# Modulation rows of a transformer layer in unsplit float32, on four 32-column tiles of the matmul array

## The chip, the cores and the metric

One core of one Trainium2 chip runs the whole kernel. A core has a matmul engine (TensorE, PE in the profile, with its weight loads as PEld), VectorE (DVE), ScalarE (ACT), GpSimd (POOL), and queues of transfers that move data between HBM and the on-chip memory SBUF; here SyncE (SP) issues nearly all transfers. Matmuls write to PSUM, which has eight banks. The metric is the time of one execution on the device in microseconds (us).

## The reference

One layer of a diffusion backbone over 256 latent tokens and 256 context tokens of width 2048, all in float32. Both token sets are normalised and modulated by scales and shifts that a large matrix makes from a conditioning vector, then projected, mixed and sent through an MLP. What concerns the change is the start:

```python
mod = (jax.nn.silu(c) @ w_mod[l] + b_mod[l])[:, None, :]
sa, ca, ga, sm, cm, gm = jnp.split(mod, 6, axis=-1)
mod_c = jax.nn.silu(c_ctx) @ w_mod[l] + b_mod[l]
sa_c, ca_c, ga_c, sm_c, cm_c, gm_c = jnp.split(mod_c, 6, axis=-1)
h_c = modulate(x_ctx, norm_attn_w[l], sa_c, ca_c)      # rmsnorm(x) * (1 + scale) + shift
h = modulate(x, norm_attn_w[l], sa, ca)
p = h @ w_in[l]                                        # Q, K, V, pooling input, gates
```

The scale and shift before attention (`ca`, `sa`) are needed for both conditioning vectors: 2048 x 4096 weights by two vectors. `ga`, `sm`, `cm`, `gm` are needed for the latent tokens alone and are made later on VectorE. After the projection come attention of 8 heads with two softmaxes each, a pooling branch, gates, an output projection with a residual, and an MLP of width 8192.

## The kernel before, in words

Float32 operands of most matmuls are split in two: ScalarE rounds a weight chunk to the reduced format float32r (`whi`, L213), VectorE subtracts (`wlo`, L214), and three matmuls at the speed of the reduced format (hi by hi, lo by hi, hi by lo) replace one in full float32 (`mm3`, L241 to L243; `xstat`, L410 to L413). A chunk is 128 x 1024 numbers, 512 KB. It lands in one of five `raw` buffers (`raw_chunk`, L113), and the next transfer into that buffer is issued when its last reader is through.

`plan` writes down one list of all chunks, the stream; `wchunk` takes the next and has `load_next` bring chunks from it `ahead` places early. Each engine runs its own instructions in order; a scheduler interleaves them at build time.

The front of the program goes as follows. The tokens `xT` land; sums of squares (L459 to L461: square on ScalarE, add, a float32 matmul with a constant) give the norms. Then come the modulation weights `w_m`, in feature groups `m` of 256 features (the first in two halves). `mod_chunk` (L347) takes a chunk: the stationary operand is `cv`, 128 columns wide, of which four are not zero (hi and lo of the two conditioning vectors), and the moving operand is 512 columns of `whi`, then of `wlo`. After all of K = 2048, `mod_rows` (L352) copies four rows out of PSUM, `mod_columns` turns them into columns by transposes (L359), copies those (L361), adds hi and lo (L365) and applies biases and the norm's weight (L367 to L369). `hidden` (L380 to L382) makes the modulated tokens of that group, `hL` for latent and `hC` for context tokens, as hi and lo.

While modulation chunks stream in, the first half of the K and Q projections runs beside them as side work: `first_steps` yields three matmuls at a time, and the table `carried` says at which chunk of which group the K chunk for latent tokens ("kx"), for context tokens ("kc") or the Q chunk ("q") is begun. When all 16 feature tiles are done, the rest of K and Q follows, and then V (`xstat`), with the evacuations `qk_evac` beside it. Behind that stand the second half of Q, K and V, pooling, gates, attention (its score matmuls at L646, its products with V at L674), the output projection and the MLP. None of these is touched.

Of the kernel before, what the change touches and what calls it, by code (L numbers as in the profile page):

```python
# [11 lines left out]
F32 = mybir.dt.float32  # L12
F32R = mybir.dt.float32r
# [35 lines left out]
def layer(ctx: ExitStack, tc, a, out):  # L49
# [74 lines left out]
    def plan(name, *idx, rate=0.0):  # L124
# [3 lines left out]
    carried = {1: ((1, "kx", 0), (4, "q", 0)), 2: ((2, "kx", 1), (4, "q", 1)),  # L128
               3: ((0, "kc", 0), (3, "kx", 2), (5, "q", 2), (6, "kc", 1))}
    for m in range(4, 8):  # L130
        carried[m] = ((0, "kc", m - 2), (2, "kx", m - 1), (4, "q", m - 1))
    carried[8] = ((0, "kc", 6), (0, "kx", 7), (0, "q", 7), (0, "kc", 7))
    for m in range(9):
        if m == 0:
            for half in range(2):
                for i in range(4):
                    plan("w_m0", half, i)
        for i in range(8 if m > 0 else 0):
            if m < 8:
                plan("w_m", m - 1, i)  # L140
            for at, n, j in carried[m]:
                if at == i and n != "kc":
                    plan("w_k" if n == "kx" else "w_q", 0, j)
            if m == 1 and i > 5 or m == 2 and i < 2:
                plan("cT", (8 * m + i - 14))
            if m == 3 and i == 4:
                plan("prq")
# [29 lines left out]
    AHEAD = 2  # L177
    x1s = []
# [10 lines left out]
    def load_next():  # L189
# [14 lines left out]
        raw = raw_chunk(src, n)  # L204
        if key[:2] == ("w_k", 0):
# [134 lines left out]
    def mod_chunk(key, i, ps, n):  # L340

        hi, lo = wchunk(*key, i)
        per = 1024 // n
        for part in (hi, lo):
            for kk in range(per):
                k = per * i + kk
                pe.matmul(ps[:, 0:n], cv[:, k, :], part[:, kk * n:kk * n + n], start=(k == 0 and part is hi),  # L347
                          stop=(k == 15 and part is lo))

    def mod_rows(ps, n=512):  # L350
        rows = work("rows", [4, n])
        act.copy(rows, ps[0:4, 0:n])  # L352
        return rows

    def mod_columns(k, rows, n=2):
# [10 lines left out]
        ks = slice(k, k + n)  # L366
# [97 lines left out]
    kept = {}  # L464
    fb = {}

    def first_steps(n, j):
# [4 lines left out]
        if n == "kc":  # L472
            hi, lo = kept.pop(j)
        else:
            hi, lo = wchunk(w, 0, j)
            if n == "kx":
                kept[j] = hi, lo
# [7 lines left out]
    def steps(g, n):  # L485
        for _ in range(n):
            next(g, None)
# [5 lines left out]
    cols = {}  # L493
    for half in range(2):
        ps = bank("mod")
        for i in range(4):
            mod_chunk(("w_m0", half), i, ps, 256)
            if half == 1 and i == 1:
                cols[0] = mod_columns(0, rows, 1)
                hidden(0, 0, cols[0], 1)  # L500
        rows = mod_rows(ps, 256)
# [590 lines left out]
```

## Time and profile before

| what | value |
|---|---|
| median of 3 runs | 1520.16 us (1519.46 to 1521.07) |
| the profiled execution's own time | 1519.78 us |
| its span, first to last instruction | 1517.7 us |
| granted TensorE clock, mean | 0.994 |
| moved between HBM and SBUF | 347.82 MB, mean 229 GB/s |

The profile is of one execution. "Busy" is the time in which an engine had at least one instruction under way; matmuls overlap one another, so PE's busy time is more than what it streams. A group's row names the line, the engine, the operation, output from inputs, shape and type, then the count, the busy time and the mean length of one in ns, then the engine's idle time before such instructions with what ended it. The line of a helper stands for all that call it. A row of a wait names the waiting engine and line, what it waited for, the total, the number of times and the longest.

### The profile page before, as it was taken

To read this page: it belongs to the slowest core of one execution; us is meant where nothing else is said; L and a number is where in the kernel's file an instruction comes from. 1 tells how busy PE (TensorE), PEld (TensorE's weight loads), DVE (VectorE), ACT (ScalarE), POOL (GpSimd) and SP (SyncE) were. 2 spreads that over 40 slices of the span, in tenths; PEclk is the share of its full clock that TensorE was granted. 3 is DMA by queue.
4 is the path that set the end of the run, shared out by engine and by line. 5 is a ranking of instruction groups with operands and counts; after the bars stand their busy time and mean duration, and the time that the engine had idled before them with its cause. 6 is when DMAs were issued, how large, how long until landed. Compare 5 with 4: busy or idle time off the path is not lost.

```text
span 1517.7 us, 19767 instructions
## 1 busy us (share of the span) xinstructions
PE 1480.7 (98%) x7336; PEld 1232.8 (81%) x7336; DVE 1063.2 (70%) x1280; ACT 755.7 (50%) x1007; POOL 129.3 (9%) x124
## 2 busy tenths in 40 slices
PE   7899999999989999999999999999999999999998
PEld 5677877768878888888879988888888888888887
DVE  7799878777887767666757665666666555555675
ACT  6677534556655444444444554544444454444432
POOL 0100111000140000000000100100000000000170
PEclk9899999999999999999999999999999999999999
DMA  8888668556568787788755677767777666666664
GB/s 314 310 283 308 214 215 285 177 167 193 167 216 300 254 275 272 242 295 296 235 181 168 220 251 245 232 217 244 231 241 240 202 188 193 193 187 193 184 200 142
DMA packets 97439, 347.82 MB, mean 229 GB/s; under 512 B 11072, under 2 KB 11712, under 8 KB 97344
## 3 DMA queue, kind: packets, MB, share of 16 engines
q1 hardware_dynamic: 96768, 345.49, 70.4%
q8 instruction: 57, 0.93, 0.3%
q0 software_dynamic: 576, 1.08, 0.2%
q14 instruction: 38, 0.31, 0.1%
HBM read 344.44 MB, written 2.10 MB: 228 GB/s over the span
## 4 chain that ended last, share of the span: by engine, by line
PE 88%; issue 3%; DVE 3%; DMA 3%; ACT 1%; POOL 1%; DVEq 0%; SPq 0%; ACTq 0%; POOLq 0%
PE f L939 14%; PE f L411 8%; PE f L410 8%; PE f L413 8%; PE f L942 7%; PE pg L413 4%; PE pg L410 4%; PE pg L411 4%; PE pyy L410 2%; PE wo L410 2%; PE wo L413 2%; PE wo L411 2%; PE pyy L413 2%; PE pyy L411 2%; PE v L411 2%
## 5 line engine op out<-in xcount | busy, mean ns | idle before, releaser
L214 DVE TENSOR_TENSOR wlo<-raw,whi 128x1024 fp32r<-128x1024 f32 x507 | 628.6, 1244 | 365.2 <-ACT whi L213 350.9
L213 ACT CAST whi<-raw 128x1024 fp32r<-128x1024 f32 x507 | 529.8, 1047 | 587.3 <-PE f L411 178.1
L939 PE MATMUL f<-h,whi 128*128 128x512 f32 x896 | 224.2, 392 | 0.0
L411 PE MATMUL f<-whi,act 128*128 128x512 f32 x512 | 199.3, 389 | 0.0
L410 PE MATMUL f<-whi,act 128*128 128x512 f32 x512 | 199.3, 389 | 0.0
L939 PEld LDWEIGHTS f<-h,whi 128*128 128x128 f32 x896 | 161.5, 189 | 29.1
L588 DVE SCALAR_TENSOR_TENSOR macc<-raw,sil,macc 128x1024 f32<-128x1024 f32 x128 | 166.2, 1299 | 1.4 <-DMA raw<-in_w_cm_dram 0.8
L413 PE MATMUL f<-wlo,act 128*128 128x512 f32 x512 | 136.8, 389 | 0.0
L942 PEld LDWEIGHTS f<-h,wlo 128*128 128x128 f32 x896 | 122.2, 190 | 8.7
L942 PE MATMUL f<-h,wlo 128*128 128x256 f32 x896 | 124.9, 282 | 0.0
L413 PEld LDWEIGHTS f<-wlo,act 128*128 128x128 f32 x512 | 96.1, 188 | 20.0
L411 PEld LDWEIGHTS f<-whi,act 128*128 128x128 f32 x512 | 96.1, 188 | 19.8
L410 PEld LDWEIGHTS f<-whi,act 128*128 128x128 f32 x512 | 96.1, 188 | 19.8
L410 PE MATMUL pg<-whi,hL 128*128 128x512 f32 x256 | 100.5, 393 | 0.0
L411 PE MATMUL pg<-whi,hL 128*128 128x512 f32 x256 | 99.7, 389 | 0.0
L950 POOL TENSOR_TENSOR rsq<-relu 128x512 f32<-128x512 f32 x28 | 29.2, 1042 | 537.6 <-ACT relu L949 516.7
L413 PE MATMUL pg<-wlo,hL 128*128 128x512 f32 x256 | 68.6, 390 | 2.5 <-DVE wlo L214 2.5
L413 PEld LDWEIGHTS pg<-wlo,hL 128*128 128x128 f32 x256 | 48.0, 188 | 12.9 <-DVE wlo L214 2.9
L410 PEld LDWEIGHTS pg<-whi,hL 128*128 128x128 f32 x256 | 48.1, 188 | 10.1 <-issue 0.2
L411 PEld LDWEIGHTS pg<-whi,hL 128*128 128x128 f32 x256 | 48.1, 188 | 10.1 <-issue 0.2
L410 PE MATMUL wo<-whi,mix 128*128 128x512 f32 x128 | 49.9, 390 | 0.0
L411 PE MATMUL wo<-whi,mix 128*128 128x512 f32 x128 | 49.8, 389 | 0.0
(267 smaller groups left out, 2205.1 us busy)
## 6 DMA issues: line engine op xcount, KB each, us to landing
raw<-in_w_ff_dram SPq DMA_DIRECT2D x240, 512.0 KB, 4.3
raw<-in_w_m_dram SPq DMA_DIRECT2D x64, 512.0 KB, 4.9
raw<-in_w_ga_dram SPq DMA_DIRECT2D x32, 512.0 KB, 4.6
raw<-in_w_cm_dram SPq DMA_DIRECT2D x32, 512.0 KB, 4.6
raw<-in_w_gb_in_dram SPq DMA_DIRECT2D x32, 512.0 KB, 4.5
raw<-in_w_ga_in_dram SPq DMA_DIRECT2D x32, 512.0 KB, 4.4
raw<-in_w_sm_dram SPq DMA_DIRECT2D x32, 512.0 KB, 4.7
raw<-in_w_o_dram SPq DMA_DIRECT2D x32, 512.0 KB, 4.6
```

Source lines behind the costliest of these rows:

```text
L213: act.copy(hi, raw)
L214: vec.tensor_sub(lo, raw, hi.bitcast(F32))
L410: pe.matmul(banks[t], tok(h, k, 0, tt), wt, start=k == 0, stop=False)
L411: pe.matmul(banks[t], tok(h, k, 1, tt), wt, start=False, stop=False)
L413: pe.matmul(banks[t], tok(h, k, 0, tt), wt, start=False, stop=k == 2 * nk - 1)
L588: pin(vec.scalar_tensor_tensor(acc, raw, sil[:, 0, k:k + 1], acc, ALU.mult, ALU.add))
L939: pe.matmul(ps, hi[:, kk * P:kk * P + P], both(h2, k), start=k == 0, stop=False)
L942: pe.matmul(ps[:, T:2 * T], lo[:, kk * P:kk * P + P], act_slice(h2, k, 0), start=False, stop=k == KT - 1)
L950: gp.tensor_mul(sq, r, r)
```

## The change

The scale and shift weights are no longer split. `load_next` hands the `raw` chunk itself to the matmuls for `w_m`, and `mod_half` multiplies it in full float32. The layout on the host gives every feature tile `f` (128 features, scale and shift side by side, 256 columns) four chunks of four K tiles each. The four K tiles of a chunk go to four tiles of the array: tile `j` has 32 stationary columns (two of them not zero, one per conditioning vector), writes PSUM partitions 32j to 32j + 31, and sums over its own quarter of K. The four partial sums are added when the rows are turned: `mod_columns` multiplies the 128 rows by `quads`, a 128 x 2 matrix of ones at rows 32j + c, in place of the transposes and of the addition of hi and lo. `mod_rows` copies all 128 partitions.

Two feature tiles still share a group of columns, except at the start and the end (f = 0, 1, 14, 15), which are turned one by one. The order of the side work is written anew: one generator over K and Q pieces (`order`), advanced by `steps` at four places of each group, and `hold` takes the K and Q chunks from the stream ahead of the steps that use them. Modulation chunks are asked for three places ahead in place of two. The adds of the context tokens' squares move from GpSimd to VectorE.

```diff
-    for m in range(9):
-        if m == 0:
-            for half in range(2):
-                for i in range(4):
-                    plan("w_m0", half, i)
...
+    for m in range(1, 8):
+        kq = (("w_k", 0, m - 1), ("w_q", 0, m - 1))
+        if m == 3:
+            besides[7, 1] = kq
+        else:
+            besides[2 * m, 1], besides[2 * m, 3] = kq[:1], kq[1:]
+    for f in range(KT):
+        for i in range(4):
+            plan("w_m", f, i)
+            for key in besides.get((f, i), ()):
+                plan(*key)
+    plan("w_k", 0, 7)
+    plan("w_q", 0, 7)
...
+    FIRST_AHEAD = 3
...
+        if key[0] == "w_m":
+            loaded.append((key, raw, raw))
+            return
...
-    cv = s8("cv", [P, KT, P], F32R)
-    vec.memset(cv.bitcast(F32), 0.0)
-    silk = sil.rearrange("p a k -> p k a")
-    act.copy(cv[:, :, 0:2], silk)
-    vec.tensor_sub(cv[:, :, 2:4], silk, cv[:, :, 0:2].bitcast(F32))
+    cv = s8("cv", [P, 4, KT, 32])[:, 0]
+    vec.memset(cv, 0.0)
+    vec.tensor_copy(cv[:, :, 0:2], sil.rearrange("p a k -> p k a"))
+    quads = pool.tile([P, 2], F32, tag="quads", name="quads")
+    vec.reduce_sum(quads, ident.rearrange("p (j c) -> p c j", j=4)[:, 0:2, :], axis=AX.X)
...
-        hi, lo = wchunk(*key, i)
-        per = 1024 // n
-        for part in (hi, lo):
-            for kk in range(per):
-                k = per * i + kk
-                pe.matmul(ps[:, 0:n], cv[:, k, :], part[:, kk * n:kk * n + n], start=(k == 0 and part is hi),
-                          stop=(k == 15 and part is lo))
+        raws = [wchunk("w_m", f, 2 * half + i, ahead=FIRST_AHEAD)[0] for i in range(2)]
+        c = (f % 2) * T
+        for i in range(2):
+            for j in range(4):
+                k = 8 * half + 4 * i + j
+                pe.matmul(ps[32 * j:32 * j + 32, c:c + T], cv[:, k, :], raws[i][:, j * T:j * T + T],
+                          start=k < 4, stop=k >= 12)
...
-        for i in range(2 * n):
-            pe.transpose(pt[:, 4 * i:4 * i + 4], rows[:, i * P:i * P + P], ident[0:4, 0:4])
-        ms = small("ms", 16)
-        act.copy(ms[:, 0:8 * n], pt[:, 0:8 * n])
-        m3 = ms[:, 0:8 * n].rearrange("p (i c) -> p i c", c=4)
+        for i in range(n):
+            for a in range(2):
+                o = 2 * (a * n + i)
+                pe.matmul(pt[:, o:o + 2], rows[:, (2 * i + a) * P:(2 * i + a) * P + P], quads,
+                          start=i + a == 0, stop=i == n - 1 and a == 1, skip_group_check=True)
         col = small("col", 8)
+        act.copy(col[:, 0:4 * n], pt[:, 0:4 * n])
...
-        vec.tensor_add(c3, m3[:, :, 0:2], m3[:, :, 2:4])
...
+        mod_half(f, 0, ps)
+        n = 1 if m == 1 else 2
+        cols[f - n] = mod_columns(f - n, before, n)
+        hidden(f - n, 0, cols[f - n], n)
+        if m != 3:
+            hold("w_k", m - 1)
...
+        steps(4 if m > 2 else 0)
+        mod_half(f, 1, ps)
+        if m != 3:
+            hold("w_q", m - 1)
...
+        steps(4 if m == 3 else 3)
+        mod_half(f + 1, 0, ps)
...
+        mod_half(f + 1, 1, ps)
...
+        if m < 7:
+            steps(4 if m == 3 else 2)
+            before = mod_rows(ps, 0, 2)
+    columns(ps, 15, 1)
+    hidden(15, 0, cols[15], 1)
+    hold("w_k", 7)
+    hold("w_q", 7)
+    steps(2)
...
+    steps(100)
```

On PE, around the turn of the columns for the last full group (m = 7), the instructions stood like this before (`mod` is the PSUM bank of the rows, `modT` that of the turned columns, `first` a K chunk, w_k with a number one of the four K banks, hL and hC with a number are halves of the modulated tokens):

```order
L347 MATMUL mod<-whi,cv 128x512 x2
L347 MATMUL mod<-wlo,cv 128x512 x2
L359 MATMUL modT<-prm,rows 128x4 x4
L241 MATMUL w_k_315<-first,hC_97 128x512
L242 MATMUL w_k_315<-first,hC_97 128x512
L243 MATMUL w_k_315<-first,hC_97 128x512
L347 MATMUL mod<-whi,cv 128x512 x2
L347 MATMUL mod<-wlo,cv 128x512 x2
L241 MATMUL w_k_314<-first,hC_97 128x512
```

and stand like this now:

```order
L351 MATMUL mod<-raw,cv 32x256 x4
L365 MATMUL modT<-quads,rows 128x2 x4
L351 MATMUL mod<-raw,cv 32x256 x4
L240 MATMUL w_k_254<-first,hL_96 128x512
L240 MATMUL w_k_255<-first,hL_96 128x512
L240 MATMUL w_k_256<-first,hC_98 128x512
L351 MATMUL mod<-raw,cv 32x256 x4
L240 MATMUL w_k_257<-first,hC_98 128x512
L241 MATMUL w_k_254<-first,hL_96 128x512
L242 MATMUL w_k_254<-first,hL_96 128x512
```

One chunk was two pairs of 512 columns, one on `whi` and one on `wlo`; it is now one row of four calls of 256 columns on `raw`, each on 32 columns of the array. K and Q matmuls on the whole array stand between most of these rows, as before: the 64 chunks lie in 48 separate pieces.

At the end of the front PE had this before, up to the first V matmul:

```order
L347 MATMUL mod<-wlo,cv 128x512 x2
L241 MATMUL w_q_365<-whi,hL_95 128x512
L242 MATMUL w_q_365<-wlo,hL_95 128x512
L243 MATMUL w_q_365<-whi,hL_95 128x512
L241 MATMUL w_k_315<-first,hC_97 128x512
L242 MATMUL w_k_315<-first,hC_97 128x512
L243 MATMUL w_k_315<-first,hC_97 128x512
L241 MATMUL w_k_314<-first,hC_97 128x512
L359 MATMUL modT<-prm,rows 128x4 x4
```

and has this now, after its last chunk:

```order
L351 MATMUL mod<-raw,cv 32x256 x4
L241 MATMUL w_k_257<-first,hC_98 128x512
L242 MATMUL w_k_257<-first,hC_98 128x512
L365 MATMUL modT<-quads,rows 128x2 x2
L240 MATMUL w_k_254<-first,hL_96 128x512
L240 MATMUL w_k_255<-first,hL_96 128x512
L240 MATMUL w_k_256<-first,hC_98 128x512
L240 MATMUL w_k_257<-first,hC_98 128x512
L241 MATMUL w_k_254<-first,hL_96 128x512
```

Behind the last chunk stood 48 K and Q matmuls, and V's first ones were placed between them; now 38 stand there, without V between them.

More of the change, by code (lines that the diff above doesn't have):

```diff
@@ L483, in first_steps, with steps, hold, columns @@
                 yield
-    def steps(g, n):
-        for _ in range(n):
-            next(g, None)
+    order = [("kx", 0), ("q", 0), ("kx", 1), ("q", 1), ("kc", 0), ("kc", 1), ("kx", 2), ("q", 2)]
+    for j in range(3, 8):
+        order += [("kc", j - 1), ("kx", j), ("q", j)]
+    side = chain(*(pair_steps(*o) for o in order + [("kc", 7)]))
+    def steps(n):
+        for _ in range(n):
+            next(side, None)
+    def hold(w, j):
+        held[w, j] = wchunk(w, 0, j, ahead=FIRST_AHEAD)
+    cols = {}
+    def columns(ps, f, n):
+        cols[f] = mod_columns(f, mod_rows(ps, f, n), n)
     sb = bank("ssq")
@@ L492, in layer @@
     rms = [rsq(sb[:, 0:T], T, P / D, "aT")]
[L493 to L501, printed above, removed]
+    ps = bank("mod")
+    for f in range(2):
+        mod_half(f, 0, ps)
+        if f == 1:
+            columns(ps, 0, 1)
+            hidden(0, 0, cols[0], 1)
+        mod_half(f, 1, ps)
+    before = mod_rows(ps, 1, 1)
     for m in range(1, 8):
+        f = 2 * m
         ps = bank("mod")
@@ L538, in layer @@
+    for i in range(2):
+        hidden(14 + i, 1, cols[14 + i], 1)
+    steps(100)
     kb, qb = fb["w_k"], fb["w_q"]
```

102 lines of the change are left out of this document (37 added, 65 removed).

## The prediction, made before the changed kernel had run

> **What bounds the kernel now.** I read the page's first section, then busy time by stretches of the front (where the change lies), then the queue's waits and the groups of that part.
>
> ```profile
> core 0: 1517.7 us, clock 0.994
> PE 1480.7 (98%) x7336; PEld 1232.8 (81%) x7336; DVE 1063.2 (70%) x1280; ACT 755.7 (50%) x1007; POOL 129.3 (9%) x124
> ```
>
> PE is busy nearly all the time, so what the front ends earlier, the whole ends earlier: nothing else sets the pace behind it. In the front the picture differs (columns: stretch, length, busy time and instructions of PE, PEld, DVE, ACT, POOL, clock, DMA share, GB/s):
>
> ```profile
> 0.00:13.00 13.00, 5.32 (x17) 4.00 (x17) 5.68 (x14) 8.88 (x14) 1.82 (x6) 1.00 0.87 317
> 13.00:42.00 29.00, 24.68 (x124) 17.99 (x122) 23.59 (x33) 19.22 (x25) 0.00 (x0) 1.00 0.92 327
> 42.00:51.00 9.00, 6.25 (x16) 2.66 (x14) 5.92 (x11) 5.66 (x11) 1.09 (x1) 0.69 0.96 373
> 51.00:60.00 9.00, 8.69 (x31) 6.99 (x31) 8.74 (x6) 7.73 (x10) 6.14 (x4) 0.74 0.70 216
> 60.00:100.00 40.00, 38.98 (x172) 30.63 (x171) 36.93 (x75) 28.73 (x40) 0.00 (x0) 1.00 0.83 276
> 100.00:155.00 55.00, 54.10 (x238) 41.83 (x237) 50.23 (x71) 39.44 (x51) 0.00 (x0) 1.00 0.88 305
> 38.00:48.00 10.00, 7.17 (x24) 3.57 (x22) 4.54 (x8) 4.70 (x7) 0.00 (x0) 0.87 1.03 413
> ```
>
> The queue's longest wait up to 155 us, and the two costliest groups up to 172 us (count, busy us and mean ns, idle before and its releaser):
>
> ```profile
> SPq L113 <- DVE wlo L214: 76.3, 55, 3.6
> L214 DVE TENSOR_TENSOR wlo<-raw,whi 128x1024 fp32r<-128x1024 f32 x75 | 93.1, 1259 | 16.9 <-ACT whi L213 16.4
> L213 ACT CAST whi<-raw 128x1024 fp32r<-128x1024 f32 x75 | 77.7, 1047 | 29.2 <-DVE wlo L214 8.4 <-DMA raw<-in_w_m_dram 7.3 <-PE mod L347 5.8
> ```
>
> From 60 to 155 us DVE has work for 87.2 of 95 us, the queue waits 76.3 us in all for a raw buffer that L214 must release, and transfers run at 276 to 305 GB/s although ten microseconds at 413 occur. PE looks full (93.1 of 95), but its durations overlap. What it really streams:
>
> ```profile
> L347 PE MATMUL mod<-wlo,cv 128*128 128x512 f32 x112 | 37.3, 414 | 2.1 <-DVE wlo L214 1.8
> L347 PE MATMUL mod<-whi,cv 128*128 128x512 f32 x112 | 37.2, 413 | 3.1 <-ACT whi L213 3.0
> L347 PE MATMUL mod<-wlo,cv 128*128 128x256 f32 x32 | 5.9, 307 | 2.3 <-DVE wlo L214 2.1
> 154.75 0.62 PE L347 MATMUL mod<-wlo,cv 128*128 128x512 f32 x2
> 170.31 0.39 PE L241 MATMUL w_k<-first,hC 128*128 128x512 f32 x1
> 170.76 0.39 PE L243 MATMUL w_k<-first,hC 128*128 128x512 f32 x1
> 170.99 0.39 PE L410 MATMUL v<-whi,hC 128*128 128x512 f32 x1
> L410 PE MATMUL v<-whi,hL 128*128 128x512 f32 x6 | 2.3, 390 | 0.0
> L411 PE MATMUL v<-whi,hL 128*128 128x512 f32 x6 | 2.3, 389 | 0.0
> L413 PE MATMUL v<-wlo,hL 128*128 128x512 f32 x4 | 1.1, 389 | 0.0
> ```
>
> In an unbroken run, starts lie (170.99 - 170.31) / 3 = 0.227 us apart for 512 columns; 0.16 us of each 0.39 is overlapped. The last modulation matmul is streamed at 154.75 + 2 x 0.227 = 155.2 us. The K and Q work of the front ends at 171.0; 16 matmuls of V were slipped in before that (6 + 6 + 4), 3.6 us, so the front proper ends at **167.4 us**. By bare streaming PE would have reached 155.2 far sooner: 12.9 us of start, 224 x 0.227 + 64 x 0.114 = 58.1 of modulation, 240 x 0.227 = 54.5 of K and Q, some 6 of the rest, in all 131.5. So some 24 us there are waits, for DVE and ACT as the rows name them.
>
> **The change part by part.** *The splits.* All 64 modulation chunks lose their cast and subtraction: 64 x 1.259 = 80.6 us of DVE and 64 x 1.047 = 67.0 us of ACT. DVE's 125.4 us between 13 and 155 fall to some 45. Off DVE's path this is worth nothing in itself; its worth is that raw buffers are no longer released by DVE but by PE, and that PE's waits for L214 go. What is late next is PE or the transfers.
>
> *The matmuls.* Each chunk becomes four float32 matmuls of 256 columns, one per 32-column tile, 256 calls. The trace has float32 calls, and calls on tiles, though none on column tiles (rows of the timeline: start us, length us):
>
> ```profile
> 293.46 1.89 PE L674 MATMUL ob<-aT,v 128*128 128x256 f32 x8
> 255.52 0.39 PE L413 MATMUL k<-wlo,hL 128*128 128x512 f32 x1
> 255.75 0.61 PE L413 MATMUL k<-wlo,hC 128*128 128x512 f32 x2
> 256.29 1.13 PE L646 MATMUL sc<-kT,qT 64*128 64x512 f32 x4
> 256.29 0.30 PEld L646 LDWEIGHTS sc<-kT,qT 64*128 64x128 f32 x4 [0.35 <-issue]
> 257.35 0.42 PEld L447 LDWEIGHTS qkT<-prm,qm 128*128 128x128 f32 x4 [0.76 <-issue]
> ```
>
> L674 issues four calls and the trace shows eight matmuls: a float32 call is two passes, each (1.89 - 0.38) / 7 = 0.216 us for 256 columns, 0.38 being one pass as recorded (0.216 and the overlapped 0.16). One after another, a chunk would cost 8 x 0.216 = 1.73 us, against 4 x 0.227 = 0.91 now. L646 issues two calls of 512 columns on two halves of the rows: four passes of 0.43 us one by one would take 0.10 + 4 x 0.43 + 0.16 = 1.98 us; the row says 1.13, which is 0.10 + 2 x 0.43 + 0.16. Row tiles do run side by side, both passes. From the nearest row I take the same for columns: two rounds, **0.43 us a chunk**, 64 x 0.43 = 27.5 us for 58.1 before. The other end is 1.73 us a chunk. A middle: only neighbours overlap (a tile's second pass beside the next tile's first), 0.86 us.
>
> The Trainium skill's page "TensorE: Matmul & The Clock Gate", Part 2, says that matmuls stay in program order and only weight loads are pulled ahead; with both passes of a call adjacent that would make the middle case, and the 1.13 us row speaks against it. Its Part 3 gives 2.38 times for three column tiles of 512; at that efficiency a chunk would be an estimated 0.54 us and the sum 7 us larger.
>
> *The switches.* Around the tiled matmuls PE pauses: the second of the two L413 starts at 255.97 and is streamed by 256.20, the next weight load is at 256.29 and takes 0.10 before columns can move; behind, the last pass is streamed at 257.25 (257.42 less 0.16), the load is at 257.35 and again takes 0.10. That is 0.39 us for in and out. The new order has the 64 chunks in 48 separate pieces between other matmuls: 48 x 0.39 = 18.7 us. Below, this cost could be nothing (the pauses may belong to these waits, not to tiles); I take the row.
>
> *The turn.* Sixteen pairs of columns now come from 32 float32 calls (64 passes, each with a 128-column weight load, 0.10 us by the last row above): 6.4 us, for 32 short ones before, some 2 to 3 us. The second evacuation add on DVE goes; 0.16 us each, covered.
>
> *Order and transfers.* Transfers up to the last modulation chunk are the same 45.6 MB (64 + 7 + 7 chunks, 8 pieces of x and ctx, 0.524 MB each, and 0.5). Piece A, to the 24th modulation chunk: 36 loads, 19.0 MB, at 350 GB/s (between the 327 and 373 of the second and third stretch) 54 us and 2 of lead; PE has 12.9 + 24 x 0.43 + 13 pieces x 0.39 + 42 K and Q matmuls x 0.227 + 3.5 of sums of squares + 1.6 = 43 us, so the transfers set **56 us**. The stretch from 42 to 51, in which PE stood for POOL's sums of ctx, goes too: these are DVE's now. Piece B, chunks 25 to 64: 40 x 0.43 + 35 x 0.39 + 208 x 0.227 + 4.4 = **82.5 us** of PE; 26.5 MB take 76 us at 350. Two microseconds for waits that remain (chunk by chunk PE meets whichever is later): last chunk done at **140.5**. Behind it stand 38 K and Q matmuls, 8.6 us, the turn, 0.4, and some 2 us because the last K chunk lands and is split (1.05 + 1.26) and the last columns are made while only ten matmuls cover; hw, hL and the copies are:
>
> ```profile
> 156.97 0.57 ACT L352 COPY rows<-mod 4x512 f32<-4x512 f32 x1
> L380 DVE SCALAR_TENSOR_TENSOR hw<-xT,col,aT 128x256 f32<-128x256 f32 x16 | 7.1, 479 | 0.2
> L382 DVE SCALAR_TENSOR_TENSOR hL<-hw,col,hL 128x256 fp32r<-128x256 f32 x16 | 8.1, 541 | 0.0
> ```
>
> Front's end: 140.5 + 11 = 151.5, for 167.4. **Sum: 15.9 us less**; the profiled execution's own 1519.78 us become 1503.9, and since the median is 0.4 us above it, I say **1504 us**. Behind the front no instruction changes; V, the late modulation rows and the rest keep their order.
>
> **The rivals.**
>
> *Neighbours only* (0.86 us a chunk). For: an in-order reading of passes. Against: 1.13 us for L646. Piece A stays with the transfers, 56 (PE 53); piece B gains 40 x 0.43 = 17 us, 100; the front ends at 169: about 1521, no change.
>
> *Column tiles one after another* (1.73). For: no column tile is in the trace, and each would read the same 128 rows, where L646's tiles read different ones. Place: PE in the front; it decides once a chunk costs over 0.86. Piece A is then PE's, 43 + 24 x 1.3 = 74; B 82.5 + 40 x 1.3 = 134.5; the end 221.5, 54 us later: **1574 us**, slower.
>
> *Transfers stay at 305 GB/s*, as between 100 and 155. For: five buffers, and a chunk that waits in PE's order holds one. Against: in that stretch the queue waited for L214. A 64, B 87, end 164: 1517.
>
> *Switches free.* Transfers then set both pieces, at 373 GB/s 53 and 71, end 137: 1490.
>
> **How the numbers follow.** Four side by side 0.65 (with free switches as its lower part), transfers slow 0.11, neighbours 0.12, one after another 0.12. The likeliest case's own range is 1490 to 1514. To hold 8 in 10 the range takes in the slow transfers and half of the neighbours: 1490 to 1523. A change within 0.2% (3 us) can't be told from none. Faster: 0.65 + 0.11 + 0.03 = 0.79; same 0.05; slower 0.16 (0.12 and a third of the neighbours).
>
> **What would show it.** The modulation group should have 512 matmuls in two rounds of four, four starting within hundredths of a microsecond and 0.22 us later four more. L214 should count 11 in place of 75 up to the front's end, the queue's waits should name PE's mod, and GB/s up to the last chunk should be about 330. The first V matmul should come near 152 us. Wrong would be: starts of tiles 0.2 us apart (neighbours) or 0.4 us apart (one by one); pauses at the 48 pieces far from 0.4 us; GB/s near 300 with PE idle; or a front 16 us shorter and an end that isn't, which would mean that PE isn't the bound behind it.

## The result, and the profile after

The changed kernel takes **1546.92 us** (median, 1544.86 to 1549.12) where the kernel before takes 1519.81 in the same comparison: a ratio of 1.0178, with a 95% interval of 1.016 to 1.0195. It is slower by 27 us; the forecast was 1504, in a range up to 1523. The forecast's direction and its time are both wrong. A few executions in the comparisons below took two to three times as long as the others (2994 to 4056 us) and are left out.

The page of the changed kernel (span; then PE, PEld, DVE, ACT, POOL with busy time, share of the span and instructions):

```profile
span 1543.3 us, 20017 instructions
PE 1498.7 (97%) x7592; PEld 1200.3 (78%) x7592; DVE 987.3 (64%) x1215; ACT 691.3 (45%) x944; POOL 120.5 (8%) x120
```

PE was busy for 1480.7 us and is now busy for 1498.7, although it streams fewer columns. That alone says that something other than the modulation has become dearer. The stretches of the front, in the columns that the prediction used (stretch, length, busy time and instructions of PE, PEld, DVE, ACT, POOL, clock, DMA share, GB/s):

```profile
13.00:42.00 29.00, 22.47 (x176) 11.22 (x168) 6.74 (x18) 6.05 (x13) 0.00 (x0) 0.76 1.01 389
42.00:51.00 9.00, 4.94 (x25) 1.98 (x29) 6.89 (x10) 6.54 (x12) 0.00 (x0) 0.50 0.64 234
51.00:60.00 9.00, 9.00 (x53) 5.81 (x53) 0.48 (x2) 0.98 (x2) 0.00 (x0) 0.94 0.87 279
60.00:100.00 40.00, 40.00 (x288) 24.48 (x286) 18.59 (x55) 11.48 (x22) 0.00 (x0) 1.00 0.88 312
100.00:155.00 55.00, 46.77 (x285) 25.73 (x281) 17.89 (x42) 13.30 (x25) 0.00 (x0) 0.84 0.74 251
```

DVE and ACT have lost some 60% of their work there. PE has not gained by it: from 100 to 155 us it stands for 7 us more than before, its clock is 0.84 where it was 1.00, and the transfers fall from 305 to 251 GB/s. The groups up to 172 us, the queue's longest waits up to 155 us, the modulation's matmuls up to 61.2 us, and rows of PE's timeline (start, length, with the count of matmuls in one row):

```profile
L351 PE MATMUL mod<-raw,cv 128*32 128x256 f32 x512 | 43.9, 435 | 4.5 <-DMA raw<-in_w_m_dram 4.5
L213 DVE TENSOR_TENSOR wlo<-raw,whi 128x1024 fp32r<-128x1024 f32 x11 | 13.5, 1223 | 7.9 <-ACT whi L212 7.8
SPq L113 <- PE mod L351: 83.9, 52, 4.4
SPq L113 <- DVE first L213: 13.9, 4, 3.7
L351 PE MATMUL mod<-raw,cv 128*32 128x256 f32 x192 | 17.8, 480 | 4.5 <-DMA raw<-in_w_m_dram 4.5
12.72 1.72 PE L351 MATMUL mod<-raw,cv 128*32 128x256 f32 x28
157.19 0.64 PE L351 MATMUL mod<-raw,cv 128*32 128x256 f32 x8
170.57 0.39 PE L242 MATMUL w_k<-first,hC 128*128 128x512 f32 x1
170.80 0.40 PE L414 MATMUL v<-whi,hL 128*128 128x512 f32 x1
171.50 0.40 PE L415 MATMUL v<-whi,hL 128*128 128x512 f32 x1
```

The tiles do run side by side: 28 passes lie in 1.72 us, that is seven rounds of four with (1.72 - 0.38) / 6 = 0.22 us from one to the next. But the last chunk comes at 157.2 us and the K and Q work of the front ends at 170.8, where V now begins. Before, with V's early matmuls taken off, it ended at 167.4. So the loss has two parts: the **front** is 3.4 us longer instead of 15.9 shorter, and **what stands behind it** takes 1543.3 - 170.8 = 1372.5 us where it took 1517.7 - 167.4 = 1350.3, 22 us more, with the same instructions.

The second part is spread over the matmuls of 512 columns behind the front that read `whi` or `wlo`. One of the large groups there, in the kernel before:

```profile
L410 PE MATMUL f<-whi,act 128*128 128x512 f32 x512 | 199.3, 389 | 0.0
```

and the same statement in the changed kernel:

```profile
L414 PE MATMUL f<-whi,act 128*128 128x512 f32 x512 | 202.7, 396 | 0.0
```

Each matmul is recorded 7 ns longer, and the starts of successive ones lie 233 ns apart in place of 227, at the full clock; V's first ones show it already, (171.50 - 170.80) / 3 = 0.233 us. In the built program one thing differs behind the front: `quads`, a new tile of 8 bytes per partition, which takes 32, stands ahead of `tabs`, `raw`, `whi` and `wlo`. `whi` begins at byte 200192 of each partition where it began at 200160; `hL`, `act` and the other large tiles stay where they were (132320 and so on).

The first part shows in PE's waits from 12 to 172 us and in the timeline at the third of those stops (start, length, engine, line; in brackets the idle time ahead and what ended it):

```profile
PE w_k L240 <- ACT first L212: 15.1, 6, 3.9
98.94 0.17 ACT L368 COPY col<-modT 128x8 f32<-128x8 f32 x1 [2.31 <-PE modT L365]
99.40 0.64 PE L351 MATMUL mod<-raw,cv 128*32 128x256 f32 x8
100.11 0.91 ACT L385 ACTIVATE hL<-hw,col 128x256 fp32r<-128x256 f32 x2 [1.01 <-DVE hw L384]
100.93 0.49 ACT L385 ACTIVATE hC<-hw,col 128x256 fp32r<-128x256 f32 x1
101.33 1.03 ACT L212 CAST first<-raw 128x1024 fp32r<-128x1024 f32 x1
102.41 0.73 PE L240 MATMUL w_k<-first,hL 128*128 128x512 f32 x2 [2.36 <-ACT first L212]
```

Six times PE has done all that was ready and stands until ACT has cast the next K chunk, 15.1 us in all. The cast needs nothing but its data, yet here it stands in ACT's order behind the `hL` and `hC` of the group, which wait for the turn. What follows each stop (stretches after the stops at 100 and 119 us):

```profile
103.30:106.70 3.40, 3.40 (x14) 1.70 (x13) 2.51 (x6) 1.14 (x2) 0.00 (x0) 0.50 0.57 165
106.70:118.90 12.20, 12.20 (x93) 6.93 (x92) 0.12 (x1) 0.75 (x2) 0.00 (x0) 1.00 0.78 273
120.40:127.20 6.80, 5.03 (x18) 2.55 (x18) 4.51 (x8) 3.16 (x5) 0.00 (x0) 0.50 0.64 213
```

The granted clock is halved for 3.4 or 6.8 us, and PE, now late, releases the raw buffers late: 165 and 213 GB/s. The Trainium skill, "TensorE: Matmul & The Clock Gate", Part 1, has the clock go to half after an idle window of some 3.4 us. The lengths of the slow stretches agree with such windows; the stops that bring them here are shorter than one, 2.4 and 2.9 us.

### The profile page after: what moved, and what is told of

Read it like the earlier page. It is cut to its first block, busy times and chain, and to the rows that moved or that the text cites. A ratio compares the mean times of both kernels' runs of the same rounds, so it can differ in the third digit from the quotient of the medians.

```text
span 1543.3 us, 20017 instructions
## 1 busy us (share of the span) xinstructions
PE 1498.7 (97%) x7592; PEld 1200.3 (78%) x7592; DVE 987.3 (64%) x1215; ACT 691.3 (45%) x944; POOL 120.5 (8%) x120
## 3 DMA queue, kind: packets, MB, share of 16 engines
q0 software_dynamic: 576, 1.08, 0.2%
## 4 chain that ended last, share of the span: by engine, by line
PE 94%; DVE 2%; ACT 2%; POOL 1%; DMA 1%; issue 1%; DVEq 0%; SPq 0%; ACTq 0%; POOLq 0%
PE f L966 14%; PE f L414 8%; PE f L417 8%; PE f L415 8%; PE f L969 7%; PE pg L417 4%; PE pg L415 4%; PE pg L414 4%; PE mod L351 2%; PE wo L415 2%; PE pyy L415 2%; PE v L417 2%; PE pyy L417 2%; PE wo L417 2%; PE v L415 2%; PE v L414 2%
## 5 line engine op out<-in xcount | busy, mean ns | idle before, releaser
L213 DVE TENSOR_TENSOR wlo<-raw,whi 128x1024 fp32r<-128x1024 f32 x443 | 547.5, 1237 | 377.7 <-ACT whi L212 361.3
L212 ACT CAST whi<-raw 128x1024 fp32r<-128x1024 f32 x443 | 462.6, 1045 | 594.1 <-PE f L415 188.1
L414 PE MATMUL f<-whi,act 128*128 128x512 f32 x512 | 202.7, 396 | 0.0
L415 PE MATMUL f<-whi,act 128*128 128x512 f32 x512 | 201.7, 394 | 0.0
L417 PE MATMUL f<-wlo,act 128*128 128x512 f32 x512 | 140.2, 395 | 0.0
```

Source lines behind the costliest of these rows:

```text
L212: act.copy(hi, raw)
L213: vec.tensor_sub(lo, raw, hi.bitcast(F32))
L414: pe.matmul(banks[t], tok(h, k, 0, tt), wt, start=k == 0, stop=False)
L415: pe.matmul(banks[t], tok(h, k, 1, tt), wt, start=False, stop=False)
L417: pe.matmul(banks[t], tok(h, k, 0, tt), wt, start=False, stop=k == 2 * nk - 1)
```

## The experiments on the place in memory

In all runs "front" and "behind" are worked out as above, from the last K or Q matmul of the front. The kernel before was at 1519.8 to 1520.6 us in each comparison.

**Quads padded to 64 bytes.** The order of all instructions is as in the changed kernel.

```
-    quads = pool.tile([P, 2], F32, tag="quads", name="quads")
+    quads = pool.tile([P, 16], F32, tag="quads", name="quads")[:, 0:2]
```

> The changed kernel with the tile quads 64 bytes long per partition in place of 8 (8 take 32 in memory), nothing else: the order of all engines is the same. Everything that lies behind it in SBUF (small tiles, tables, norms, raw, whi, wlo) then starts at 32 modulo 64 bytes, as in the kernel before; in the changed kernel it starts at 0. Theory A (place in memory): matmuls of 512 columns go from 232 to 234 ns start to start back to 227, the part behind the front from 1372 to 1350 us, the front itself shrinks by a few us at most, in all about 1522 to 1526 us. Rival B (what follows the front is slow because of what the front did to the clock or the order): no change, 1545 to 1549 us.

Measured 1526.85 us, ratio 1.0046 (1.003 to 1.0063): 20 us come back from 56 more bytes of empty room, by which `whi` moves on by 32. Front 171.0, behind 1352.4. So the place counts, and the 16 us expected in the front are missing for another reason.

**The kernel before, moved by 32 bytes.**

```
+    gap = pool.tile([P, 2], F32, tag="gap", name="gap")
+    vec.memset(gap, 0.0)
     b1 = small("b1", 16)
```

> The kernel before with one idle tile of 8 bytes per partition put between sil and the small tiles, so that raw, whi and wlo start at 0 modulo 64 bytes instead of 32; no instruction differs except one memset of that tile. Theory A: matmuls slow from 227 to 233 ns, about 22 us behind the front and 3 in it: 1541 to 1547 us. Rival B: 1520 us as before.

Measured 1543.82 us, ratio 1.0157 (1.0137 to 1.0177). Behind the front 1374.0 us, the front 166.0, no longer than before. The group of above in this run:

```profile
L412 PE MATMUL f<-whi,act 128*128 128x512 f32 x512 | 202.7, 396 | 0.0
```

The same loss without any part of the change. That settles the cause of the second part: the place. What about the place it is that counts was not yet clear.

**All tiles moved by 32 bytes**, the same tile ahead of every other one:

```
+    gap = pool.tile([P, 2], F32, tag="gap", name="gap")
+    vec.memset(gap, 0.0)
     prm = pool.tile([P, PRM_W], F32, tag="prm", name="prm")
```

> The kernel before with a tile of 8 bytes ahead of every other tile: all tiles move by 32 bytes, the weights in work (whi, wlo) and the stationary tiles (hL, hC, act) alike, so that both start on multiples of 64; nothing else moves. Theory: the place of the moving operand alone decides: 512 columns 233 ns apart as with the weights alone moved, and the whole near 1543 us. Rival: what counts is how the moving and the stationary operand stand to each other: both have moved alike, so 227 ns and 1520 us.

Measured 1520.22 us, ratio 0.9999 (0.9989 to 1.0009), and the group stands as in the kernel before:

```profile
L412 PE MATMUL f<-whi,act 128*128 128x512 f32 x512 | 199.3, 389 | 0.0
```

The rival held. `whi` now stands at 200192 exactly as in the slow kernels, and is fast, because the stationary tiles moved with it; the idle tile's memset is in both runs and costs nothing. So it is the distance between the tiles that counts, not the address of one.

**Raw alone by 32, whi and wlo by 64.** The gap of the kernel moved by 32 bytes, and a second one behind the first buffer of `raw`:

```
         raw = pool.tile([P, n], F32, tag="raw", name="raw", bufs=5)
+        if not loaded:
+            vec.memset(pool.tile([P, 2], F32, tag="gap2", name="gap2"), 0.0)
```

> The kernel before with 32 bytes ahead of the five buffers of raw and 32 more between them and whi: only the buffers into which the transfers write start on multiples of 64, whi and wlo stand at 32 beyond one, as before. Theory: the matmul reads whi and wlo, so their place decides: 227 ns, 1520 us. Rival: the place of the buffers that the transfers fill slows the reads of the matmuls beside them: 233 ns, about 1543 us.

Measured 1523.74 us, ratio 1.0027 (1.0018 to 1.0037), which is neither 1520 nor 1543:

```profile
L414 PE MATMUL f<-whi,act 128*128 128x512 f32 x512 | 200.0, 391 | 0.0
```

This 391 is what the run with quads at 64 bytes has as well, where `raw` had moved by 64. In both `whi` and `wlo` stand 64 bytes off. So it makes no difference here whether the buffers that the transfers fill have moved by 32 or by 64, and 64 bytes are not free: they cost these matmuls 2 ns each.

**Longer gaps.** First quads at 128 bytes (`pool.tile([P, 32], ...)[:, 0:2]`), then the kernel before with gaps of 96 and 256 bytes (`pool.tile([P, 24], ...)` and `[P, 64]` for the `gap` ahead of `b1`):

> The changed kernel with quads padded to 128 bytes in place of 64: raw, whi and wlo stand 128 bytes behind their place in the kernel before. With 64 the matmuls of 512 columns behind the front were 229 ns apart, with 32 some 233, with none 227. Theory: what counts is the distance of the two operands' start addresses taken modulo 128, so 128 is as none: 227 ns, the part behind the front 1350.4 us as in the kernel before, and the whole near 1525 us. Rival: modulo 64, the 229 of before are something else: 1527 us.

> The kernel before with 96 bytes ahead of raw, whi and wlo where 32 made it 1543.8 us. Theory: the distance of the operands modulo 128, and 96 lies as far from a multiple as 32: 233 ns, about 1543 us. Rival: each further 32 bytes takes the loss down in its own step, 64 having cost 2 us: between 1520 and 1530 us.

> The kernel before with 256 bytes ahead of raw, whi and wlo. 32, 96 and 128 gave 1544 to 1545 us, 64 gave 228.9 ns and some 1522.5, none 1520. Theory: the place counts modulo 256 (all starts of whi, wlo, hL and act are alike modulo 256 in the kernel before): 227 ns, 1520 us. Rival: it counts over a longer distance: 229 to 235 ns, 1524 to 1545 us.

Measured 1545.08 us for 128 (1.0164; 1.0149 to 1.0179), 1545.18 for 96 (1.0159; 1.0142 to 1.0176), and 1520.67 for 256 (1.0004; 0.9995 to 1.0013). The group with 128 bytes:

```profile
L414 PE MATMUL f<-whi,act 128*128 128x512 f32 x512 | 202.0, 395 | 0.0
```

and with 256:

```profile
L412 PE MATMUL f<-whi,act 128*128 128x512 f32 x512 | 199.4, 390 | 0.0
```

My theory of 128 bytes fell: it had foretold the 96 and failed on the 128. With 256 the kernel is as fast as with none, and in the kernel before `whi`, `wlo`, `raw`, `hL` and `act` all begin at the same place modulo 256. Six distances were tried: 0 and 256 are fast, 64 costs 0.2 to 0.3% of the whole, 32 and 96 cost 1.6%, and 128 costs 1.4% (against the run with quads in cv's tile, below).

`whi` and `wlo` have moved not only against the other operand of each matmul, but also against all that the other engines read and write. The traces tell these apart. Among the matmuls of `f` on `act` and `pg` on `hL`, those during which no other engine and no transfer had anything under way (15 and 16 of them) lie 226.7 ns apart in the kernel before and 233.3 in the changed one, as the rest do. So the loss is in what PE itself reads, and not in traffic beside it. It does not hold for every shape: the 256-column matmuls of `f` with `wlo` as the stationary operand lie 119 ns apart with a distance of 0 or 32 bytes, and 114 with 64. Nor is it all: the K matmuls of the front, on `first` and `hL`, neither of which had moved, went from 229 to 231 ns in the kernel moved by 32 bytes.

What inside the chip makes it so, and whether the period is 256 in general, stays open. The Trainium skill, "TensorE: Matmul & The Clock Gate", Part 2, gives PE two independent read ports into SBUF, one for the streamed operand and one for the weights. The runs show that the distance of the two operands counts all the same, and not why.

**Quads in a free part of cv's tile**, so that nothing is allocated:

```
-    cv = s8("cv", [P, 4, KT, 32])[:, 0]
+    cvs = s8("cv", [P, 4, KT, 32])
+    cv = cvs[:, 0]
-    quads = pool.tile([P, 2], F32, tag="quads", name="quads")
+    quads = cvs[:, 1, 0, 0:2]
```

> The changed kernel with the two columns of quads in a part of cv's tile that nothing uses: nothing is allocated for them, so raw, whi and wlo stand where they stood in the kernel before. Theory: only their place cost the 22 us behind the front: 227 ns between matmuls of 512 columns, 1350 us behind the front, the front at 171 to 172 us, the whole near 1524 us. Rival: something else of the change slows the matmuls: more than 1360 us behind the front.

Measured 1523.46 us, ratio 1.0028 (1.0016 to 1.0039); behind the front 1349.2, the front 170.6. The whole change on the modulation, with all places as before, is thus worth 3 us in the wrong direction, and all of it lies in the front.

## The experiments on the front

These stand on the kernel with quads at 64 bytes (1526.85 us) unless something else is said.

**The K chunks' cast on POOL.**

```
-        act.copy(hi, raw)
+        if key[:2] == ("w_k", 0):
+            gp.tensor_copy(hi, raw)
+        else:
+            act.copy(hi, raw)
```

> e1_pad64 with the casts of the first eight K chunks on GpSimd in place of ScalarE, where they stood behind the tokens' activations. Theory C (PE's stops of 2.4 to 4.5 us at the first K matmul of a group, which wait for that cast, hold the front up, directly and by the lower clock that follows each): the stops go, the front ends near 150 us in place of 168 to 171, total 1500 to 1508 us. If the stops only move (the subtraction of the same chunk waits on VectorE next, or the cast on GpSimd takes 2 us and more) 1515 to 1525. Rival D (PE is limited by transfers or by the switches between tiles and the whole array): within 3 us of e1_pad64.

Measured 1521.14 us, ratio 1.0006 (0.9995 to 1.0017), 5.7 us less; the front ends at 167.4. PE's waits now:

```profile
PE w_k L243 <- ACT hL L388: 4.3, 3, 1.8
PE w_k L244 <- DVE first L216: 3.1, 4, 1.2
PE w_k L243 <- ACT hC L388: 1.7, 1, 1.7
PE w_k L243 <- POOL first L213: 1.6, 2, 1.3
```

The waits for the cast were real, 15.0 us of them in the run that this one stands on. With the cast off ACT, `hL`, `hC` and the subtraction on DVE are what comes last, 9.1 us in all, and POOL's cast itself for 1.6 more: the stops move there.

**Zeros ahead of four K chunks.** A zeroed piece of cv's tile is the stationary operand; the products are zeros added to a sum in progress.

```
+        if n == "kx" and j in (1, 4, 5, 6):
+            for _ in range(6):
+                pin(pe.matmul(fb["w_q"][0][:, 0:T], nought, xT[:, 0, :], start=False, stop=False))
```

> e1_pad64 with six float32 matmuls of a zero matrix, 2.6 us, put at four of the stops (before K chunks 1, 4, 5 and 6 for latent tokens), adding zeros to a Q bank: they run where PE would stand, and keep it active. If the lower clock behind each stop is a cost of its own, the clock stays at 1.0 from 100 us on, the front ends 8 to 12 us sooner than in e1_pad64 although PE has 10 us more work. If the clock costs nothing, or the stops remain as long as before with the work added, the front ends 0 to 10 us later.

Measured 1520.89 us, ratio 1.0009 (0.9996 to 1.0021): 24 calls more, some 2.6 us of PE at each of four places, and the whole is 6.0 us shorter. The stretch from 100 to 155 us, PE's wait for the cast from 12 to 172 us, and rows of PE's timeline (L482 is the zeros):

```profile
100.00:155.00 55.00, 51.98 (x348) 30.36 (x348) 20.06 (x49) 14.30 (x28) 0.00 (x0) 1.00 0.83 276
PE w_k L240 <- ACT first L212: 8.6, 5, 3.8
104.34 0.74 PE L240 MATMUL w_k<-first,hL 128*128 128x512 f32 x2 [1.90 <-ACT first L212]
107.74 2.86 PE L482 MATMUL w_q<-xT,cv 128*128 128x256 f32 x12
118.57 1.05 PE L368 MATMUL modT<-quads,rows 128*128 128x2 f32 x8
121.95 0.40 PE L241 MATMUL w_k<-first,hC 128*128 128x512 f32 x1
```

Clock 1.00 in place of 0.84 and 276 GB/s in place of 251. But the zeros do not run where PE stops: those at 107.74 begin 3.4 us after the stop has ended. What helps is the order that came with them. Between the turn at 118.57 and the next K matmul on `hL` PE now has nine K matmuls of the other side (the row at 121.95 is the last but one), where the run without zeros has none, and so the stop there is 0.6 us long in place of 2.9. The waits for the cast fall by 6.4 us (from 15.0), and the zeros add 10.4 us of work. By these two alone the front would end 4 us later; it ends 4.3 us sooner (166.7 for 171.0), so by this estimate some 8 us are the clock's. The lower clock is thus a cost of its own, and with the stops shortened it did not come. That zeros as such keep it up is not shown, here or in the next run.

**Both together**, with three calls of zeros at each place:

> The changed kernel with quads padded to 64 bytes, the cast of the K chunks on POOL, and before the first K matmul of chunks 1, 4, 5 and 6 three float32 matmuls of zeros (1.3 us) into an accumulation, which leave its sums as they are. The two apart took 5.7 and 6.0 us off 1526.9. Theory: the wait for the cast and the lower clock behind it are two costs: together some 9 us less, 1517 to 1518 us. Rival: both only take the same lower clock away: 1521 us, as each alone.

Measured 1519.66 us, ratio 0.9994 (0.9985 to 1.0003). Together 7.2 us, more than either alone and less than their sum: in part they take away the same stops.

**The two chunks of a half together.** In `mod_half`, from column block 6 on, the chunk that lands last is taken first, so that the scheduler places the other's matmuls right behind it: 33 pieces in place of 49, so 16 fewer where I had expected 15.

```
-        for i in range(2):
+        turns = (1, 0) if f >= 6 else (0, 1)
+        for n, i in enumerate(turns):
...
-                          start=k < 4, stop=k >= 12)
+                          start=half + n == 0, stop=half + n == 2)
```

> The changed kernel with quads padded, where from column block 6 on the two chunks of a half are taken in the other order (the one that comes last first), so that their eight matmuls stand together: 20 pieces in place of some 35. Theory: behind chunk 24 PE's own work sets the pace and each switch costs it 0.39 us: 15 fewer are 5.9 us less, 1521 us. Rival: the wait for the cast and the buffers set the pace, and switches lie in idle time: 1526 to 1528 us; with each first chunk's buffer held until the second has come, up to 1531.

Measured 1521.00 us, ratio 1.0000 (0.9991 to 1.0009): 5.85 us less, which for 16 pieces would be 0.37 us each. The front ends at 162.4. Two kinds of stop stay:

```profile
PE w_k L240 <- ACT first L212: 5.8, 2, 4.0
PE w_k L240 <- ACT hL L386: 5.3, 3, 1.8
```

Since the stops changed too (11.1 us of them for 15.0), 0.37 is not a clean price of a switch. The timeline of the changed kernel has one:

```profile
95.01 0.40 PE L241 MATMUL w_k<-first,hC 128*128 128x512 f32 x1
95.33 0.64 PE L351 MATMUL mod<-raw,cv 128*32 128x256 f32 x8
95.90 0.50 PE L242 MATMUL w_k<-first,hC 128*128 128x512 f32 x1
96.25 0.40 PE L240 MATMUL w_k<-first,hC 128*128 128x512 f32 x1
```

From 95.01 to 96.25 lie two K matmuls, 0.47 us, and one chunk, 0.43; the 0.34 us that remain are the way into the tiles and out. The 24 chunks of the changed kernel that stand alone like this at the full clock have 0.34 in the median.

**Pairs and the cast on POOL, without and with zeros**, on quads at 128 bytes, by the theory that had just been made:

> The changed kernel with quads padded to 128 bytes, the two chunks of a half together from column block 6 on, and the cast of the K chunks on POOL. The pairs alone were at 1521.0 with two of three stops left to the hL activation and one of 4.0 us to the cast. Theory: the cast's stop goes (3 us) and the place of the weights gives 2 us: 1516 us. Rival: on POOL the cast is out of the way already where the pairs moved it, only the place is left: 1519 us.

> As the run with pairs and the cast on POOL, with three float32 matmuls of zeros (1.3 us) before the first K matmul of chunks 1, 4, 5 and 6, which leave the sums as they are. Theory: the stops of 1.8 us for hL still halve the clock for 3.4 to 6.8 us each, and the fill keeps it: 3 to 4 us less than without, 1512 to 1513 us. Rival: the fill takes as much as it gives (5.2 us of matmuls against some 7 us of lost clock): within 1 us of the run without.

Measured 1538.25 us (1.0117; 1.0102 to 1.0132) and 1541.06 (1.0134; 1.0117 to 1.0151). Against 1545.08 with 128 bytes alone the first is 6.8 us better; the place of the weights hides it. The zeros bring nothing here: 2.8 us more by medians of four and three executions, 1.1 us more by the profiled spans. The timeline of PE in the run with zeros shows why they do not help:

```profile
117.34 1.05 PE L372 MATMUL modT<-quads,rows 128*128 128x2 f32 x8
120.26 1.19 PE L243 MATMUL w_k<-first,hL 128*128 128x512 f32 x2 [1.86 <-ACT hL L392]
```

They run ahead of the turn, and the stop that counts stands behind it, from the turn over `col` to `hL`. It is 1.86 us long with and without them, since this time no K matmuls were left behind the turn. Work that is to cover a stop has to stand inside it.

**The turn early.** With quads in cv's tile, pairs, and from column block 8 on the turn and `hL` ahead of the next half's matmuls; first with the cast on POOL, then on ScalarE:

```
+        if m < 4:
+            mod_half(f, 0, ps)
         cols[f - n] = mod_columns(f - n, before, n)
         hidden(f - n, 0, cols[f - n], n)
+        if m >= 4:
+            mod_half(f, 0, ps)
```

> The changed kernel with quads in cv's tile, the two chunks of a half together from column block 6 on, the cast of the K chunks on POOL, and from the eighth column block on the turn and what follows it ahead of the next half's matmuls, so that hL is in work while PE still has matmuls of the half and of K's other side. Theory: PE's last stops (1.9 us each, and the halved clock behind each) stand on the chain rows, turn, col, hL: they go, the front ends by 158 to 160 us, the whole 1511 to 1513 us. Rival: the transfers set the pace then: the front not before 163 us, 1516 us.

> As the run with the turn early, but with the cast of the K chunks on ScalarE, as the change has it. Theory: without the stop of 4 us at 43 us and the cast's wait behind hL the front would end sooner; with it 2 to 3 us later than with the cast on POOL, 1514 to 1516 us. Rival: with hL early the cast stands in no one's way: the same time as on POOL.

Measured 1518.40 us (0.9991; 0.998 to 1.0002) and 1518.71 (0.9994; 0.9985 to 1.0002), both some 5 us better than with quads in cv's tile alone, and alike: where the cast runs no longer matters. The pairs alone had given 5.85, so putting the turn early brought nothing on top. The first one's front ends at 165.2, far from the 158 to 160 that I expected. PE's waits from 60 us on:

```profile
PE w_k L244 <- DVE first L216: 5.1, 5, 1.8
PE w_k L243 <- POOL first L213: 2.9, 2, 1.5
PE w_k L243 <- ACT hL L390: 1.1, 1, 1.1
```

The stop for `hL` is nearly gone, and the K chunk's own arrival, with its cast and subtraction, has taken its place.

**The K chunk asked for two chunks sooner, without and with zeros** (three calls of zeros ahead of `kx` of the chunks 3 to 6):

```
-            besides[2 * m, 1], besides[2 * m, 3] = kq[:1], kq[1:]
+            besides[(2 * m - 1, 3) if m > 3 else (2 * m, 1)], besides[2 * m, 3] = kq[:1], kq[1:]
...
         if m >= 4:
+            hold("w_k", m - 1)
             mod_half(f, 0, ps)
```

> As the run with the turn early and the cast on POOL, with the K chunk of a group asked for two weight chunks sooner (from the fourth on), since PE's stops there ended with the cast and the subtraction that the chunk's arrival sets off. Theory: the last waits for K's chunk go, the front ends at 161 to 162 us against 165.2, the whole 1514 to 1515 us. Rival: the stops move on to hL or to the weights of the modulation, which the K chunk now holds up: within 2 us of 1518.4.

> As the run with the K chunk earlier, with three float32 matmuls of zeros (1.3 us) before the first K matmul of chunks 3 to 6, which leave the sums as they are. Theory: what stops stay (some 1.5 us each) still halve the clock for 3.4 to 6.8 us, and the fill keeps it whole: 2 to 3 us less than without. Rival: with the chunk earlier there is no stop left to fill: 3 us more than without.

Without zeros 1516.66 us, ratio 0.9987 (0.9977 to 0.9998); its profiled execution has a span of 1520.3 us, longer than the median, and in it the stops have gone back to `hL`. With zeros **1513.05 us, ratio 0.9963 (0.9949 to 0.9976)**: a version faster than both kernels (by 0.4% than the kernel before). From 100 to 155 us it shows:

```profile
100.00:155.00 55.00, 49.83 (x346) 32.73 (x339) 19.57 (x49) 11.96 (x25) 3.26 (x3) 0.94 0.83 283
```

Its front ends at 162.1, and behind it are 1348.6 us. In its order one to six K matmuls of the other side stand between the turn and the first matmul on `hL`, so both the zeros and the changed order may have a part in the last 3.6 us; the runs do not tell them apart.

## Why the prediction was wrong, step by step

*Four column tiles side by side, 0.43 us a chunk:* right. Two rounds of 0.22 us, and no sign of the middle case (0.86) or of one after another (1.73). The 2.38 times that the Trainium skill gives for three tiles in "TensorE: Matmul & The Clock Gate", Part 3, would have made it an estimated 0.54; here four tiles took the time of one.

*The splits:* right. 11 of L214's 75 subtractions are left up to the front's end, and the queue waits for PE's `mod`, as was said under what would show it.

*The switches, 0.39 us:* right but for 0.05 us. The trace has 0.34, and 49 pieces where 48 were counted; the 5.85 us of the pairs are near what 16 of them make.

*Piece A, 56 us by transfers:* by 61.2 us the group of the modulation counts x192, 24 chunks, so the piece took 5 us longer. The timeline of the changed kernel between 42 and 49 us:

```profile
42.16 1.08 PE L351 MATMUL mod<-raw,cv 128*32 128x256 f32 x8 [0.79 <-DMA raw<-in_w_m_dram]
43.46 2.69 ACT L463 ACTIVATE sq<-cT 128x512 f32<-128x512 f32 x5
46.06 1.03 ACT L212 CAST first<-raw 128x1024 fp32r<-128x1024 f32 x1
47.14 0.80 PE L240 MATMUL w_k<-first,hL 128*128 128x512 f32 x1 [3.90 <-ACT first L212]
```

Transfers were faster than the 350 GB/s that I took as long as they set the pace (389 from 13 to 42 us). The step that failed is "the transfers set 56": PE stood 3.9 us for the second K chunk's cast, which ACT took behind five squares of ctx, and went on at half the clock, with 234 GB/s. The clock had fallen just before that stop, behind waits of under 1 us for the weights: the chunk at 42.16 takes 1.08 us, where others take 0.64. The prediction has this stretch go; PE was busy for 4.94 us of its nine, less than the 6.25 before. I had looked at the stop that the change removes there, POOL's, and not at what is late next.

*Piece B, 82.5 us of PE and two for waits:* the last chunk was done at 157.6, 96.5 us later, in place of 84.5. The stops at 100, 119 and 140 us are 2.4, 2.9 and 2.9 us long, and behind them lie 3.4, 6.8 and 6.8 us of half clock, of which PE was busy for 13.4 (3.40 and 5.03 in the rows above, 4.97 at 141 us): 6.7 us lost. That is 8.2 + 6.7 = 14.9 in place of the two microseconds that the sum allowed, and explains the 12 that are missing; PE's own work was right to within a microsecond or so. So the prediction counted the work of PE and not the order of ACT: with the modulation shorter, a group's K work is done sooner, but the chain rows, turn, `col`, `hL` and the cast behind it is as long as it was, and so PE meets it. The clock was taken as full, though the profile of before has 0.69 and 0.74 around its own stop between 42 and 60 us.

*The tail, 11 us:* 13.2 (170.8 less 157.6), with one more stop for the cast and 3.4 us of half clock.

*"Behind the front no instruction changes", so that what the front ends earlier the whole ends earlier:* this is the dearest error, 22 of the 41 us that the spans miss. No instruction changed, and each 512-column matmul on `whi` or `wlo` became 6 ns slower, because the change allocates a tile of 8 bytes. The premise was right on the order and said nothing of the operands' places.

None of the rivals was the one that came true. By the spans, 1517.7 - 15.9 = 1501.8 us were forecast and 1543.3 came: of the 41.5 us between, 22.2 lie behind the front and 19.3 in it (5.1 in piece A, 12.0 in piece B, 2.2 in the tail).

Of the front it stays open why 162 us could not be beaten. With the stops partly covered the transfers run at 283 GB/s, while the same queue reached 389 as long as it found buffers free; the queue still waits for PE's `mod`. Five raw buffers and a chunk that waits in PE's order, the condition of the rival with slow transfers, is the likeliest reason, but it was only argued.

## What to carry to other kernels

When an edit makes work on one path shorter, follow the chain that feeds its next stage (here turn, `col`, `hL`, and a cast queued behind them) and ask when PE runs out of ready matmuls; a stop of two microseconds can cost as much again in clock. Compare the built program's start addresses as well as its order: a small new tile ahead of the big ones can change the rate of the long matmuls behind it, and putting it into a free corner of a tile that exists cost nothing here (1349.2 us behind the front, for 1350.3). If all long matmuls become a few nanoseconds slower at full clock, look at the operands' places before anything else.

## What the runs showed of the hardware that was not expected

- The rate of 512-column matmuls depends on the distance between the start addresses of their operands: 227 ns where both begin at the same place modulo 256, 229 with 64 bytes between, 232 to 234 with 32, 96 or 128. Moving all tiles alike changes nothing (0.9999). With no other engine and no transfer under way it is 226.7 and 233.3 ns for 0 and 32 bytes, so other traffic is not the cause. Matmuls of 256 columns do not follow this: 119 ns at 0 and 32 bytes, 114 at 64.
- Stops of PE of 1.2 to 2.9 us were followed by stretches of 3.4 or 6.8 us at half the granted clock, though not each one: in the run with six zeros a place a stop of 1.9 us at 102 us was not. With those stops shortened the clock from 100 to 155 us was 1.00 for 0.84, worth some 8 us by the sum above.
- Four float32 matmuls on column tiles take the time of one, both passes: 0.22 us a round of four.
